# Filling projections placed step by step in a braided attention stage, by VectorE's time instead of TensorE's

## The chip, the cores and the metric

The kernel runs on one core of one Trainium2 chip. The metric is the device time of one execution in microseconds; a kernel is timed several times and the median is compared. The profile that is shown is of one execution.

## The reference, cut to what matters

One decoder layer on 1024 tokens, 16 learned meta tokens ahead of them (T = 1040), all in fp32:

```python
h = h + 0.5 * swiglu(rms_norm(h, ffn1_norm), ffn1_w_in, ffn1_w_out)
u = rms_norm(h, mix_norm) @ w_in            # one combined projection
hq, hf, hi, hg, sq, sk, sv = split(u)       # HGRN2 heads | stick-breaking heads
o_hg = hgrn2(hq, hf, hi, hg, ...)           # 4 heads, 128 x 128 state, blocks of 128
o_sb = stick_breaking(sq, sk, sv, ...)      # 8 heads of 64
h = h + concat[o_hg, o_sb] @ w_out
h = h + 0.5 * swiglu(rms_norm(h, ffn2_norm), ffn2_w_in, ffn2_w_out)
```

A stick-breaking head, for one block of 128 queries:

```python
z = einsum('qd,kd->qk', q, k) * scale
log_keep = where(allowed, log_sigmoid(-z), 0)
suffix = cumsum(log_keep, reverse=True) - log_keep
w = exp(where(allowed, log_sigmoid(z), -inf) + suffix)
o = w @ v
```

An HGRN2 head projects q, f, i (its value) and a gate g, and computes a gated linear recurrence: within a block by products of q and k with the decays between them, between blocks by a state.

## The kernel before, in words

*Stages.* FFN1, then the combined projection up to the columns that the stick-breaking heads need (to 849.5 us of the profiled execution), then the **attention stage** (849.5 to 1119.7), in which the stick-breaking heads are computed and the columns of the HGRN heads are projected between their steps, then the **HGRN stage** (to 1255.8), in which the HGRN heads run between the steps of w_out for the first half of the tokens, then the rest of w_out and FFN2. The first 28 us of the HGRN stage, up to the first w_out step at 1147.3, are the hand-over: the projections that are left over run there beside the first instructions of three heads.

*Number format.* Every big matrix product is done on fp32 operands split in a high and a low part: `product` (L242) issues three matmuls for each 128 rows of the contraction, high by high (L249), high by low (L250) and low by high (L251), into one PSUM tile. One **product step** of a projection is four such triples, 12 matmuls, 512, 256 or 272 columns wide; two steps fill one tile `proj`. A step of w_out is one triple into a tile `wo`.

*Orders.* TensorE's order is written out: it runs its instructions in the order in which the program issues them. The orders of the other engines (VectorE = DVE, ScalarE = ACT, GpSimd = POOL, and SyncE = SP, which issues most DMAs) are set by a scheduler from what the program issues.

*The attention stage.* `sb_jobs` (L1518) yields 32 jobs, 8 heads by 4 pairs of query blocks in the order 0, 6, 2, 4 (the second job of a head is its largest, with blocks 6 and 7). A job consists of three lists of steps:

- *score steps* (`sb_scores`, L1645), one for each piece of up to 456 key columns: TensorE computes `z` (L1664, L1665), ScalarE the sigmoids `keep` and `sig` (L1666, L1667), VectorE a running product over the piece, the scan (L1670), and POOL multiplies it with sig (L1677). `z` has two PSUM buffers.
- *turn steps* (`unit`, `meta`): TensorE transposes up to four 128 x 128 blocks of sig, `flip` (L1515, L1571; two PSUM buffers), and `sb_parts` splits them into a high part by a copy on ScalarE (L1642) and a low part by a difference on VectorE (L1643), tiles `wu` (and `wm` for the meta columns).
- *value steps*: matmuls of `wu` and `wm` with the values `v` into `oacc` (L1592, L1594). `sb_out` writes the job's output away.

`braid` (L1718) sets the order. In slot `at` stand the score steps of job `at`, the turns of job `at - 2` and the values of job `at - 3`. Each slot gets filling steps from `columns` (`hgrn_fill`, L1131): product steps of the HGRN heads' columns, in the order v, f, q, g of each head. Their eviction `use` takes two sigmoids on ScalarE (L1154, L1155) and two operations on VectorE for f, one each (L1162, L1163) for q and g, a copy on ScalarE for v; the results `st` are stored to DRAM (hg_v, hg_k, hg_f, hg_q, hg_g) by DMAs on SP. With a new column its weights `raw` are loaded (L227) and split by a cast on ScalarE (L232) and a difference on VectorE (L234). Before, a slot's filling is 1.22 times the slot's own time on TensorE by the planner's table; it is spread evenly over the slot's places, and every step is sorted by its place.

*The HGRN stage.* What `braid` left of `columns` goes to `rest()`, and `weave` puts the first instructions of HGRN heads between these product steps (it ends with the fill). `hgrn_attend` (L1198) loads vT, KB, QA, F and masks (L1212), turns vT on TensorE (`flip`, evicted by L1233 and L1236 into vm and vr), multiplies QA with KB for the blocks (`lvl`, L1248) into `attn` (L1252, VectorE), scales QA by F (L1249), then goes level by level: KB is multiplied with F (L1270, VectorE), ScalarE copies it into KP (L1277), TensorE multiplies QA with KP (`lvl`, L1283), and VectorE writes the result into attn by a predicated copy (L1291). Behind the levels `op` (L1347, L1351) applies attn to the values, and `onp` (L1367) turns the normed result vT back. The second `weave` puts the heads' remaining steps between the 64 w_out steps of `first_half_of_o`.

The calls in `run()`:

```python
self.braid(jobs, islice(columns, 76), 1.22, 2.0, 3.0)
...
left = list(columns)                      # in rest(): product steps that braid left over
...
self.weave(rest(), heads[:3], 1e6, 1.0, True)
```

Of the kernel before, what the change touches and what calls it, by code (L numbers as in the profile page):

```python
# [49 lines left out]
class Block:  # L50
# [1667 lines left out]
    def braid(self, jobs, fill, share, turn, value):  # L1718


        waiting = []
        owed = 0.0
        at = 0
        while True:
            job = next(jobs, None)
            for lag, steps in zip((0.0, turn, value), job or ()):
                spans = [1.0 if lag == turn else t for t, _ in steps]
                done = 0.0
                for span, (t, f) in zip(spans, steps):
                    waiting.append((at + lag + (done + span / 2) / sum(spans), t, f))  # L1730
                    done += span
            if not waiting:
                break
            now = [x for x in waiting if x[0] < at + 1]
            waiting = [x for x in waiting if x[0] >= at + 1]
            owed += share * sum(t for _, t, _ in now)
            more = []
            while owed > 0:
                step = next(fill, None)
                if step is None:  # L1740
                    break
                more.append(step)
                owed -= step[0]
            now += [(at + (i + 0.5) / len(more), t, f) for i, (t, f) in enumerate(more)]
            for _, _, f in sorted(now, key=lambda x: x[0]):
                f()
            at += 1

    def weave(self, fill, streams=(), total=0.0, work=0.0, brief=False, steady=False):

# [48 lines left out]
    def run(self):  # L1799
# [21 lines left out]
        with ExitStack() as c0:  # L1821
            with ExitStack() as c1:
# [8 lines left out]
                with tc.manual_schedule(engines={nc.tensor.engine}), ExitStack() as c2:  # L1831
# [4 lines left out]
                    turn = self.pool("turn", ctx=c2)  # L1836
# [68 lines left out]
                    def taken(at, step=True):  # L1905
# [14 lines left out]
                    steps = self.fast_in(  # L1920
                        ops, n, a["ffn1_w_in"][0], act1D, 4, ev0, open_ev, None, begin, spare,
                        lambda: next(turning[0], None), late=lambda: next(later, None),
                        taken=taken,
                    )
# [14 lines left out]
                with tc.manual_schedule(engines={nc.tensor.engine}), ExitStack() as c2:  # L1939
# [140 lines left out]
                    loads = {("A12", 7 + m): (m, c_a) for m in range(4)}  # L2080
# [54 lines left out]
                    def project_early(ci, *plan):  # L2135
                        t0, m = CHUNKS[ci]
                        banks = [early_bank(name, ci, tag) for name, _, tag in plan]
                        for k in range(KT):
                            for ps, (_, w, _) in zip(banks, plan):
                                self.product(ps, w, xh, xl, t0, m, [k])  # L2140
                            if k == 3:
                                yield
# [6 lines left out]
                    key = project_early(0, ("k", wk, None))  # L2149
# [5 lines left out]
                    value = project_early(0, ("v", wv, None))  # L2155
# [22 lines left out]
                columns = self.hgrn_fill(xh, xl, pst, hgD)  # L2178
                oH, self.att = [], []

                def tasks():
                    done = []
                    for i in range(4):
                        for x in done[i - 2] if i > 1 else ():
                            yield "join", x
                        done.append(
                            (yield from self.sb_project(i, xh, xl, mixb, mix, (qD, kD, vD)))
                        )
                        if i == 2:
                            next(jobs)  # L2190
                    for t, f in islice(columns, 16):
                        f()
                        yield t

                with tc.manual_schedule(engines={nc.tensor.engine}):
                    cf = ExitStack()
                    fetch = self.pool("fetch", ctx=cf, side="right")
                    jobs = self.sb_jobs((qD, kD, vD, oD), fetch, self.att)
                    with ExitStack() as c2:
                        mixb = self.pool("mixb", ctx=c2)  # L2200
                        mix = self.pool("mix", ctx=c2)
                        self.weave(tasks())
                    with ExitStack() as c2:
                        self.att.append(self.pool("att1", ctx=c2))
                        tag = self.proj_tags[0]
                        self.proj_tags = [self.proj_tags[1]] * 2
                        self.begin = self.pproj.tile([P, 512], F32, tag=tag, name="begin", bufs=1)
                        nc.vector.memset(self.begin, 0.0)
                        nc.vector.tensor_copy(self.begin[:, 1 : P + 1], self.ident[:, ::-1])
                        self.braid(jobs, islice(columns, 76), 1.22, 2.0, 3.0)  # L2210
                    cf.close()
                    self.proj_tags[0] = tag
                    hg_ctx = ExitStack()
                    hg = self.pool("hg", ctx=hg_ctx, side="right")
                    heads = [self.hgrn_attend(h, hg, hgD, oH) for h in range(4)]
                    self.wide = hg.tile([P, 5, 512], U8, name="wide")
                    for i, n in enumerate(LEVELS[:5]):
                        m = self.masks[:, i, :].rearrange("p (b h r) -> p b h r", h=2, r=n)
                        wide = self.wide[:, i].rearrange("p (h c x) -> p h c x", h=2, c=4)
                        for half in range(2):  # L2220
                            for c in range(4):
                                nc.vector.tensor_copy(
                                    wide[:, half, c].rearrange("p (b r) -> p b r", r=n),
                                    m[:, :, 1 - half, :],
                                )
                    for h in range(3):
                        next(heads[h])

                    def rest():
                        left = list(columns)  # L2230
                        for t, f in left[:-1]:
                            f()
                            yield t
                        left[-1][1]()

                    self.weave(rest(), heads[:3], 1e6, 1.0, True)
# [15 lines left out]
            with tc.manual_schedule(engines={nc.tensor.engine}), ExitStack() as cx:  # L2252
# [103 lines left out]
                def turn_next():  # L2356
# [3 lines left out]
                steps = self.fast_in(  # L2360
                    ops, n, a["ffn2_w_in"][0], actD, 2, ev0, open_ev, made,
                    after_opened=after_opened, between=turn_next,
                )
# [10 lines left out]
            with tc.manual_schedule(engines={nc.tensor.engine}), ExitStack() as c1:  # L2374
# [5 lines left out]
                loads = {("A12", 2 * m): (m, 0) for m in range(4)}  # L2380
# [39 lines left out]
```

## Time and profile before

| | us |
|---|---|
| median of 3 runs | 1944.56 (1943.69 to 1945.66) |
| the profiled execution | 1939.29 |
| its span in the trace | 1937.6 |
| attention stage, in the trace | 849.5 to 1119.7 |
| hand-over, up to the first w_out step | 1119.7 to 1147.3 |
| rest of the HGRN stage | 1147.3 to 1255.8 |

How to read the lines that follow. A row of the table by stage has the stretch, its length, then for PE, PEld, DVE, ACT and POOL the busy time and the count of instructions, and at the end the mean granted clock of TensorE (1.00 is full), the mean busy share of the DMA engines and GB/s. A row of the chain of waits, or of one tile's instructions, has its start, its duration, engine, source line, operation and tiles, and in brackets how long the engine had stood idle before it and for what. A row of waits, "PE flip L1515 <- DVE wu L1643: 2.1, 4, 0.9", says who waited for whom, the sum in us, how often, and the longest. A row of the costliest groups has busy time and the mean in ns of one instruction, then the idle time before them and what ended it.

### The profile page before, as it was taken

What the parts mean: (1) busy time and instruction counts of PE and PEld (TensorE: products, weight loads), DVE (VectorE), ACT (ScalarE), POOL (GpSimd) and SP (SyncE); (2) the same over time, 40 slices, a digit from 0 to 9 for tenths busy, and PEclk for the clock granted to TensorE, in tenths of its full rate; (3) what the DMA queues carried; (4) which work ended last, traced back from release to release, by engine and by line L of the source; (5) the groups of instructions that cost most, each with busy time, mean ns of one, the idle gap of its engine ahead of it and who ended that gap; (6) DMA issues with size and microseconds to landing.
All of it is one profiled execution on the core that took longest, in us unless ns stands there. A gap on an engine that the chain in (4) does not pass through costs nothing.

```text
span 1937.6 us, 30264 instructions
## 1 busy us (share of the span) xinstructions
PE 1916.0 (99%) x10637; PEld 1620.2 (84%) x10637; DVE 1393.9 (72%) x2184; ACT 847.8 (44%) x1712; POOL 452.5 (23%) x625
## 2 busy tenths in 40 slices
PE   9999999999999999999999999999999999999999
PEld 7888888888888888889998988888888888888887
DVE  7977778877678666567777776667577767767774
ACT  7523443334444544356666635433223332344443
POOL 3010100101000003133334342210545544530000
PEclk9999999999999999999999999999999999999999
DMA  7266898757966316765454178646544444469463
GB/s 220 89 174 169 249 287 252 234 190 287 383 229 189 126 53 158 173 183 150 135 155 121 59 257 245 163 186 209 172 127 134 133 128 133 129 251 318 143 233 114
DMA packets 381689, 355.55 MB, mean 184 GB/s; under 512 B 129041, under 2 KB 284561, under 8 KB 381537
## 3 DMA queue, kind: packets, MB, share of 16 engines
q1 hardware_dynamic: 360768, 288.98, 49.4%
q0 software_dynamic: 20768, 64.63, 9.6%
q8 instruction: 84, 1.38, 0.3%
q14 instruction: 69, 0.56, 0.1%
HBM read 237.95 MB, written 115.57 MB: 182 GB/s over the span
## 4 chain that ended last, share of the span: by engine, by line
PE 90%; DVE 5%; ACT 2%; DMA 1%; issue 1%; POOL 1%; SPq 0%; DVEq 0%; POOLq 0%; ACTq 0%
PE o L735 22%; PE qb L452 18%; PE qc L452 12%; PE qa L452 12%; PE proj L249 4%; PE proj L251 4%; PE proj L250 4%; PE flip L1515 2%; PE wo L250 1%; PE wo L249 1%; PE wo L251 1%; PE mq L1014 1%; PE oacc L1594 1%; PE oacc L1592 1%; PE z L1665 1%
## 5 line engine op out<-in xcount | busy, mean ns | idle before, releaser
L452 PE MATMUL qb<-T,wh 128*128 128x512 f32 x1056 | 343.8, 390 | 0.3 <-DVE u L484 0.3
L452 PEld LDWEIGHTS qb<-T,wh 128*128 128x128 f32 x1056 | 198.2, 188 | 44.4 <-issue 3.3
L452 PE MATMUL qa<-B,wh 128*128 128x512 f32 x696 | 227.6, 392 | 0.3 <-ACT B L838 0.2
L362 DVE TENSOR_TENSOR wl<-s,wh 128x512 fp32r<-128x512 f32 x160 | 166.0, 1037 | 70.0 <-ACT wh L360 69.1
L249 PE MATMUL proj<-xh,wh 128*128 128x512 f32 (+2 forms) x640 | 212.7, 332 | 1.2 <-ACT kT L1391 0.6
L735 PE MATMUL o<-t,w 128*128 128x512 f32 x924 | 211.9, 390 | 0.0
L251 PE MATMUL proj<-xl,wh 128*128 128x512 f32 (+2 forms) x640 | 209.3, 327 | 0.7 <-DVE xl L1983 0.7
L735 PE MATMUL o<-parts 128*128 128x512 f32 x924 | 209.6, 389 | 0.0
L250 PE MATMUL proj<-xh,wl 128*128 128x512 f32 (+2 forms) x640 | 208.9, 326 | 0.0
L452 PE MATMUL qb<-T,wl 128*128 128x512 f32 x528 | 205.4, 389 | 0.0
L735 PEld LDWEIGHTS o<-t,w 128*128 128x128 f32 x924 | 172.8, 188 | 36.9 <-issue 0.4
L735 PEld LDWEIGHTS o<-parts 128*128 128x128 f32 x924 | 173.4, 188 | 36.0
L360 ACT CAST wh<-s 128x512 fp32r<-128x512 f32 x160 | 99.4, 622 | 187.3 <-PE qb L452 143.7
L452 PEld LDWEIGHTS qa<-B,wh 128*128 128x128 f32 x696 | 130.5, 188 | 29.2 <-issue 1.2
L360 ACT CAST wh<-raw 128x512 fp32r<-128x512 f32 x120 | 74.4, 621 | 144.7 <-PE qc L452 96.7
L452 PE MATMUL qa<-B,wl 128*128 128x512 f32 x348 | 135.5, 389 | 0.0
L249 PEld LDWEIGHTS proj<-xh,wh 128*128 128x128 f32 x640 | 120.9, 189 | 13.0 <-ACT st L1155 1.3
L251 PEld LDWEIGHTS proj<-xl,wh 128*128 128x128 f32 x640 | 120.9, 189 | 11.7 <-DVE xl L1983 1.2
L250 PEld LDWEIGHTS proj<-xh,wl 128*128 128x128 f32 x640 | 121.1, 189 | 9.2
L452 PEld LDWEIGHTS qb<-T,wl 128*128 128x128 f32 x528 | 99.1, 188 | 20.3
L452 PE MATMUL qc<-T,wh 128*128 128x512 f32 x352 | 116.0, 391 | 0.0
L452 PE MATMUL qc<-B,wh 128*128 128x512 f32 x352 | 114.5, 389 | 0.0
(400 smaller groups left out, 3831.0 us busy)
## 6 DMA issues: line engine op xcount, KB each, us to landing
raw<-in_ffn_w_in_dram SPq DMA_DIRECT2D x176, 256.0 KB, 4.0
raw<-in_ffn_w_out_dram SPq DMA_DIRECT2D x112, 256.0 KB, 4.4
w2in<-both SPq DMA_DIRECT2D x28, 512.0 KB, 4.1
raw<-in_w_in_dram SPq DMA_DIRECT2D x25, 512.0 KB, 4.7
ks<-kD SPq DMA_DIRECT2D x32, 260.0 KB, 4.7
wout<-both SPq DMA_DIRECT2D x16, 512.0 KB, 3.7
wh<-w2in SPq DMA_DIRECT2D x27, 256.0 KB, 3.5
wl<-w2in SPq DMA_DIRECT2D x27, 256.0 KB, 3.5
```

Source lines behind the costliest of these rows:

```text
L249: nc.tensor.matmul(ps, wh[:, s], xs, start=k == 0, stop=False)
L250: nc.tensor.matmul(ps, wl[:, s], xs, start=False, stop=False)
L251: nc.tensor.matmul(ps, wh[:, s], xl[:, k, c0 : c0 + n], start=False, stop=k == nk - 1)
L360: nc.scalar.copy(hi, src)
L362: self.block_lo = nc.vector.tensor_sub(lo, src, hi.bitcast(F32))
L452: nc.tensor.matmul(ps, a[:, k, :], b[:, k, :], start=start and k == 0 and i == 0, stop=k == 3 and i == 2, skip_group_check=True,)
L735: nc.tensor.matmul(banks[bank][m], y[:, m * P : (m + 1) * P], z, start=start and at == 0 and e == 0, stop=q == nq - 1 and e == 2, skip_gro ...
L1014: nc.tensor.matmul(ps[at : at + 32, :], self.xm[:, 4 * h + k, :], got[i, h][:, k, :], start=h == 0 and k == 0, stop=h == 1 and k == 3, til ...
L1515: self.nc.tensor.transpose(ps[:m, j, :], src[:, s0 : s0 + m], self.ident)
L1592: nc.tensor.matmul(o[:, c], vj, w[0], start=j == 0, stop=False, skip_group_check=True)
L1594: nc.tensor.matmul(o[:64, c], vj[:, :64], w[1], start=False, stop=end, skip_group_check=True)
L1665: nc.tensor.matmul(z, q, ks[1][:, s0 : s0 + n], start=False, stop=True)
```

## The change

`braid` places the filling in another way. Each score step adds 70 + 2.74 t (t is the step's number in the planner's table, its columns) and each turn step 140 + 1.28 t to what is owed, times `share`; value steps add nothing. These formulas are for VectorE's time. As soon as more is owed than half of the next filling step's own time, that step follows right behind. There is no even spreading any more. What of the 76 steps is not placed when the jobs are through is issued behind the last of them. `share` goes from 1.22 to 0.9.

```diff
         owed = 0.0
         at = 0
+        step = next(fill, None)
         while True:
             job = next(jobs, None)
-            for lag, steps in zip((0.0, turn, value), job or ()):
+            loads = (lambda t: 70 + 2.74 * t), (lambda t: 140 + 1.28 * t), (lambda t: 0.0)
+            for lag, load, steps in zip((0.0, turn, value), loads, job or ()):
                 spans = [1.0 if lag == turn else t for t, _ in steps]
                 done = 0.0
                 for span, (t, f) in zip(spans, steps):
-                    waiting.append((at + lag + (done + span / 2) / sum(spans), t, f))
+                    place = at + lag + (done + span / 2) / sum(spans)
+                    waiting.append((place, share * load(t), f))
                     done += span
             if not waiting:
                 break
             now = [x for x in waiting if x[0] < at + 1]
             waiting = [x for x in waiting if x[0] >= at + 1]
-            owed += share * sum(t for _, t, _ in now)
-            more = []
-            while owed > 0:
-                step = next(fill, None)
-                if step is None:
-                    break
-                more.append(step)
-                owed -= step[0]
-            now += [(at + (i + 0.5) / len(more), t, f) for i, (t, f) in enumerate(more)]
-            for _, _, f in sorted(now, key=lambda x: x[0]):
+            for _, load, f in sorted(now, key=lambda x: x[0]):
                 f()
+                owed += load
+                while step is not None and owed > step[0] / 2:
+                    step[1]()
+                    owed -= step[0]
+                    step = next(fill, None)
             at += 1
+        while step is not None:
+            step[1]()
+            step = next(fill, None)
...
-                        self.braid(jobs, islice(columns, 76), 1.22, 2.0, 3.0)
+                        self.braid(jobs, islice(columns, 76), 0.9, 2.0, 3.0)
```

In number, 74 product steps stood in the attention stage before and 6 were left for `rest()`. Now 75 stand between the jobs' steps, one is drained behind the last, and 4 are left. At the opening of the stage the first product step stands behind the first three score pieces (144, 272 and 456 columns); before, it stood behind the first alone.

TensorE in the middle of the attention stage, between the second and the third job of the first head. `z` are score pieces, `flip` turns, `oacc` values, `proj` products. Before:

```order
L1515 MATMUL flip_8864<-ident_65,sig_8694 128x128 x3
L1664 MATMUL z_8873<-ks_8678,qs_8677 128x144
L1665 MATMUL z_8873<-ks_8679,qs_8677 128x144
L1592 MATMUL oacc_8857<-wu_8745,v_7954 128x256
L1594 MATMUL oacc_8857<-wu_8746,v_7954 64x256
...
L1592 MATMUL oacc_8857<-wu_8779,v_7954 128x256
L1594 MATMUL oacc_8857<-wu_8780,v_7954 64x256
L1515 MATMUL flip_8886<-ident_65,sig_8725 128x128 x4
L249 MATMUL proj_8899<-xh_6535,wh_8612 128x512
```

After:

```order
L1515 MATMUL flip_8883<-ident_65,sig_8710 128x128 x3
L1664 MATMUL z_8892<-ks_8694,qs_8693 128x144
L1665 MATMUL z_8892<-ks_8695,qs_8693 128x144
L249 MATMUL proj_8834<-xh_6535,wh_8631 128x512
...
L1592 MATMUL oacc_8876<-wu_8758,v_7954 128x256
L1594 MATMUL oacc_8876<-wu_8759,v_7954 64x256
...
L1592 MATMUL oacc_8876<-wu_8795,v_7954 128x256
L1594 MATMUL oacc_8876<-wu_8796,v_7954 64x256
L1515 MATMUL flip_8921<-ident_65,sig_8738 128x128 x4
```

The product step stood behind the flip of four blocks; now it stands right behind the score piece, ahead of the values and of that flip.

TensorE at the hand-over. `flip<-vT` and `lvl` are the first instructions of the HGRN heads, told apart by the numbers of vT, QA and KB. Before:

```order
L249 MATMUL proj_12398<-xh_6535,wh_12146 128x512
...
L1515 MATMUL flip_12427<-ident_65,vT_12291 16x128
L1515 MATMUL flip_12430<-ident_65,vT_12291 128x128 x4
...
L249 MATMUL proj_12442<-xh_6535,wh_12146 128x512
...
L1248 MATMUL lvl_12455<-QA_12288,KB_12289 128x128 x4
...
L1515 MATMUL flip_12475<-ident_65,vT_12318 16x128
...
L249 MATMUL proj_12442<-xh_6535,wh_12146 128x512
...
L1283 MATMUL lvl_12647<-QA_12288,KP_12648 128x2x64 x4
L1248 MATMUL lvl_12657<-QA_12315,KB_12316 128x128 x4
...
L249 MATMUL wo_12712<-oT_12630,wh_12626 128x512
```

After:

```order
L249 MATMUL proj_12427<-xh_6535,wh_12039 128x512
...
L1515 MATMUL flip_12597<-ident_65,vT_12320 16x128
...
L1515 MATMUL flip_12612<-ident_65,vT_12347 16x128
...
L1248 MATMUL lvl_12627<-QA_12317,KB_12318 128x128 x4
L1248 MATMUL lvl_12632<-QA_12317,KB_12318 128x128 x4
L1248 MATMUL lvl_12647<-QA_12344,KB_12345 128x128 x4
L1248 MATMUL lvl_12652<-QA_12344,KB_12345 128x128 x4
L1283 MATMUL lvl_12667<-QA_12317,KP_12668 128x2x64 x4
L249 MATMUL wo_12677<-oT_12580,wh_12576 128x512
```

The two product steps that stood between the first head's flips, its lvl and the second head's flips are gone from there; both heads' flips and their lvl of QA and KB follow one another, and the first lvl of QA and KP stands behind them. In VectorE's order the same place reads, before:

```order
L1252 TENSOR_TENSOR attn_12302<-lvl_12455,ident_65 128x512
L1249 TENSOR_TENSOR QA_12288<-QA_12288,F_12290 128x1024
L1252 TENSOR_TENSOR attn_12302<-lvl_12460,ident_65 128x512
L1233 COPY vm_12331<-flip_12475 16x128
L1270 TENSOR_TENSOR KB_12289<-KB_12289,F_12290 128x2x256
```

After:

```order
L1252 TENSOR_TENSOR attn_12331<-lvl_12627,ident_65 128x512
L1249 TENSOR_TENSOR QA_12317<-QA_12317,F_12319 128x1024
L1252 TENSOR_TENSOR attn_12331<-lvl_12632,ident_65 128x512
L1252 TENSOR_TENSOR attn_12358<-lvl_12647,ident_65 128x512
L1249 TENSOR_TENSOR QA_12344<-QA_12344,F_12346 128x1024
L1252 TENSOR_TENSOR attn_12358<-lvl_12652,ident_65 128x512
L1270 TENSOR_TENSOR KB_12318<-KB_12318,F_12319 128x2x256
```

The second head's attn, QA and attn have moved ahead of the first head's KB. On SP, the store of a product step's hg_q now stands between the first head's load of vT and its load of KB.

TensorE at the end of the HGRN stage, between the last `op` and the first `onp`. Before:

```order
L1351 MATMUL op_13657<-vr_13144,attn_13145 128x128
L249 MATMUL wo_13677<-oT_12938,wh_13673 128x512
...
L249 MATMUL wo_13677<-oT_12942,wh_13673 128x512
...
L249 MATMUL wo_13677<-oT_12946,wh_13673 128x512
...
L249 MATMUL wo_13677<-oT_12950,wh_13673 128x512
...
L1367 MATMUL onp_13692<-ident_65,vT_13134 128x128 x4
L1367 MATMUL onp_13700<-ident_65,vT_13134 128x128 x4
```

After:

```order
L1351 MATMUL op_13671<-vr_13160,attn_13161 128x128
L249 MATMUL wo_13661<-oT_12903,wh_13657 128x512
L250 MATMUL wo_13661<-oT_12903,wl_13659 128x512
L251 MATMUL wo_13661<-oT_12905,wh_13657 128x512
L1367 MATMUL onp_13692<-ident_65,vT_13150 128x128 x4
L1367 MATMUL onp_13700<-ident_65,vT_13150 128x128 x4
```

Four steps of w_out stood between them; now one does.

## The prediction

> **What bounds the kernel now.** I read the page's first part and then the table by stage.
>
> ```profile
> PE 1916.0 (99%) x10637; PEld 1620.2 (84%) x10637; DVE 1393.9 (72%) x2184; ACT 847.8 (44%) x1712; POOL 452.5 (23%) x625
> 849.50:1119.70 270.20, 262.35 (x1851) 240.75 (x1850) 201.86 (x327) 179.62 (x462) 97.08 (x140) 1.00 0.45 128
> 1119.70:1147.30 27.60, 26.25 (x157) 22.54 (x157) 17.04 (x58) 8.97 (x15) 16.44 (x36) 1.00 0.89 323
> 1147.30:1255.80 108.50, 105.47 (x695) 90.59 (x694) 75.15 (x138) 54.92 (x153) 29.35 (x44) 1.00 0.75 203
> ```
>
> TensorE is busy for 1916.0 of 1937.6 us, so no change of order can win more than some 20 us in the whole kernel. The attention stage runs from 849.5 to 1119.7 us and leaves TensorE idle for 270.20 - 262.35 = 7.85 us. The hand-over to the HGRN heads (to 1147.3) leaves 1.35 us, the rest of the HGRN stage (to 1255.8) 3.03 us. Only these three stretches have another order; behind them TensorE runs on as before. The attention stage cut at its column changes:
>
> ```profile
> 849.50:858.60 9.10, 7.22 (x35) 4.94 (x33) 6.06 (x12) 6.62 (x18) 1.30 (x4) 1.00 0.82 238
> 858.60:895.00 36.40, 34.95 (x212) 30.38 (x211) 28.81 (x46) 23.09 (x60) 16.27 (x22) 1.00 0.60 154
> 895.00:940.00 45.00, 44.02 (x365) 43.23 (x363) 36.31 (x61) 33.54 (x89) 17.95 (x26) 1.00 0.52 156
> 940.00:981.00 41.00, 39.23 (x238) 34.32 (x237) 26.67 (x44) 23.59 (x59) 12.73 (x22) 1.00 0.53 138
> 981.00:1025.00 44.00, 43.51 (x351) 41.92 (x350) 34.67 (x58) 31.96 (x85) 15.82 (x22) 1.00 0.46 130
> 1025.00:1066.00 41.00, 40.33 (x247) 35.15 (x246) 30.52 (x49) 26.69 (x71) 16.92 (x26) 1.00 0.47 135
> 1066.00:1112.00 46.00, 45.80 (x373) 44.50 (x372) 35.98 (x58) 31.26 (x81) 15.89 (x19) 1.00 0.17 57
> 1112.00:1119.70 7.70, 7.30 (x48) 6.30 (x47) 2.83 (x6) 2.87 (x7) 0.19 (x2) 1.00 0.13 46
> ```
>
> Idle are 1.88 us at the opening, 0.40 in the last 7.7 us and 5.56 between. The stretches whose products are 512 columns wide (858.6, 940, 1025) lose 3.89 of these 5.56. What TensorE waits for there:
>
> ```profile
> PE flip L1515 <- DVE wu L1643: 2.1, 4, 0.9
> PE z L1664 <- ACT sig L1667: 1.9, 4, 0.6
> PE flip L1515 <- POOL sig L1677: 1.6, 2, 1.0
> PE flip L1515 <- DVE wm L1643: 1.0, 2, 0.8
> ```
>
> The waits for wu and wm, and behind POOL's sig the scan, are VectorE that has fallen behind; no single wait is over 1.0 us.
>
> **The change, part by part.**
>
> *A, the middle of the attention stage.* VectorE's work there, by groups of instructions:
>
> ```profile
> L1670 DVE TENSOR_TENSOR_SCAN keep<-keep,begin 128x144 f32<-128x144 f32 (+6 forms) x112 | 97.6, 873 | 12.6 <-ACT keep L1666 8.0 <-POOL keep L1659 1.9 <-ACT sig L1667 1.5
> L1643 DVE TENSOR_TENSOR wu<-flip,wu 128x512 fp32r<-128x512 f32 (+2 forms) x96 | 51.9, 541 | 16.4 <-ACT wu L1642 16.0
> ```
>
> The scans cover 8 x 4736 = 37888 columns, so 2.58 ns each; the differences cover 288 blocks, so 0.18 us each. The slot with the 1952 columns of the largest job and 11 blocks costs VectorE 5.0 + 2.0 = 7.0 us, the slot with 416 columns and 7 blocks 1.1 + 1.3 = 2.4 us. By the planner's formulas the heavy slot got 1.22 x 4.2 = 5.2 us of products and now gets 0.9 x 7.3 = 6.6; the light one got 4.2 and now gets 2.5. Products leave the slots in which VectorE needs no time and go to those in which it is late, and each stands right behind the scan or difference that it covers. No instruction is added or taken away but for one product step (74 steps before, now 75 and one drained at the end), which comes from the stage behind. Bounds: nothing won (the products are still only 2.7 us apart at best), or all 5.56 us and the pipeline's drain behind each wait, some 8 us. I take 4.5, since the waits are short beside a product: **-4.5**.
>
> *B, the opening.* The first product moves from behind the first score piece to behind the third.
>
> ```profile
> 851.38 1.05 ACT L232 CAST wh<-raw 128x1024 fp32r<-128x1024 f32 x1 [1.99 <-DMA raw<-in_w_in_dram]
> 853.04 0.30 ACT L1667 ACTIVATE sig<-z 128x144 f32<-128x144 f32 x1
> 853.39 0.48 PE L1664 MATMUL z<-ks,qs 128*128 128x456 f32 x1 [0.43 <-ACT sig L1667]
> ```
>
> ScalarE stands behind a load of weights until 851.38, so the third piece can't start before 853.39 either way, there being two z buffers. Before, a product filled that time; now TensorE idles for some 3 us. But the product that stood there then stands behind the third piece, and the products behind it come between turns and pieces where the rest of the 1.88 us was lost. **0** (-0.8 to +1).
>
> *C, the close.* The last slots lose two 256-wide products and a 512-wide one between turns, which have two PSUM buffers. The waits of flip for wm above (0.8 at most) are the nearest rows: **+0.8** (0 to 1.5).
>
> *D, the hand-over.* One product step is spent in the attention stage and one is drained behind it. So five steps now follow one another, and none is left between the HGRN heads' first instructions.
>
> ```profile
> 1134.57 1.95 PE L1248 MATMUL lvl<-QA,KB 128*128 128x128 f32 x16
> 1136.35 0.71 PE L1515 MATMUL flip<-ident,vT 128*16 128x128 f32 x5
> 1137.74 0.66 PE L1515 MATMUL flip<-ident,vT 128*128 128x128 f32 x4 [0.68 <-ACT vr L1236]
> 1141.00 1.07 PE L1283 MATMUL lvl<-QA,KP 128*128 128x128 f32 x8
> 1147.30 0.48 PE L249 MATMUL wo<-oT,wh 128*128 128x512 f32 x1
> 1135.66 0.69 DVE L1252 TENSOR_TENSOR attn<-lvl,ident 128x512 f32<-128x512 f32 x1 [3.46 <-PE lvl L1248]
> 1136.55 1.96 DVE L1249 TENSOR_TENSOR QA<-QA,F 128x1024 f32<-128x1024 f32 x1 [0.20 <-PE lvl L1248]
> 1139.23 0.67 DVE L1270 TENSOR_TENSOR KB<-KB,F 128x512 f32<-128x512 f32 x1
> 1139.93 0.68 ACT L1277 COPY KP<-KB 128x512 f32<-128x512 f32 x1 [0.92 <-DVE KB L1270]
> 1143.09 1.31 DVE L1291 COPY_PREDICATED attn<-wide,lvl 128x512 f32<-128x512 uint8 x1
> 1144.84 1.20 DVE L1249 TENSOR_TENSOR QA<-QA,F 128x1024 f32<-128x1024 f32 x1
> ```
>
> Before, KP was there 1140.61 - 1134.57 = 6.0 us after the first lvl, and in those 6.0 us TensorE turned the second head's vT and ran a product, with one wait of 0.68. Now TensorE does both heads' lvl at once (half of the 1.95 us more) and stands before the first lvl<-QA,KP; and VectorE does the second head's attn, QA and attn (0.69 + 1.20 + 0.69) ahead of KB. KP is there 6.0 + 2.6 = 8.6 us after the first lvl, of which some 2 are covered: a wait of 6.5. The second head's KP waits for the predicated copy, two KB and ScalarE behind the first head's lvl, 0.9 + 1.3 + 0.7 + 0.7 + 0.7 = 4.3 us, over 2.6 us of wo and flips: 1.7. With 0.7 for the flips that is 8.9 in place of 1.35: +7.5. Some is given back: TensorE is then later against VectorE, and the 3.03 us it waits for up to 1255.8 shrink; with their drain I take 3.2. **+4.3** (0 to +9). On SP the store of a drained product's hg_q now stands between the load of vT and that of KB and waits for VectorE; KB, QA and F come about a microsecond later, which the five steps cover.
>
> The granted clock is 1.00 in every row above, behind waits of at most 1 us. The Trainium skill (TensorE: Matmul & The Clock Gate, "Part 1: The HAM clock gate") says that TensorE's clock is halved after an idle window of about 3.4 us and comes back after as long a busy one. No row here has such a pause, so the trace neither bears it out nor denies it; by the rows the sum stays as it is, by the rule some 1.7 us come on top, an estimate from that page.
>
> *E, the end of the HGRN stage.* With more of the heads' work in the last interleaving, its 64 wo steps run out sooner: one step instead of four stands between the last op and onp.
>
> ```profile
> 1252.06 0.39 PE L1351 MATMUL op<-vr,attn 128*128 128x128 f32 x2
> 1254.63 0.69 DVE L1361 TENSOR_TENSOR vT<-op,ss 128x512 f32<-128x512 f32 x1
> 1255.06 1.04 PE L1367 MATMUL onp<-ident,vT 128*128 128x128 f32 x8
> ```
>
> vT ends at 1255.32, and onp's second half (from some 1255.5) just doesn't wait. Three steps are 2.1 us, of which nearly all is bared: **+1.9** (0 to 2.1).
>
> Sum: -4.5 + 0 + 0.8 + 4.3 + 1.9 = +2.5 us. On the profiled execution's 1939.29 us that gives 1941.8; this execution lies 5.3 us under the median of the runs, 1944.56, on which it gives 1947.1. A measurement here tells about 0.2% (3.9 us) from no change.
>
> **The rivals.** *Faster:* the stage's waits go entirely (A -8) and the hand-over is mostly taken back, since the HGRN stage's waits are VectorE's (D +2, E +1): -5, 1939.6. For it speaks that 3.89 of the 5.56 us lie where products are widest, and those move most; against it that a wait of 6.5 us can't hide behind 3.03 us of idle time. *Slower, hand-over not taken back:* the order of wo and levels is fixed, and VectorE itself ends its dense stretch later, so D is +7.5: +5.7, 1950.3. It decides once the first lvl<-QA,KP waits over 5 us and the idle time from there to the end of the HGRN stage stays at 3. *Slower by the clock:* the pause of 6.5 us, or the 3 us at the opening, lets the granted clock fall; if it is halved for as long as the long pause was, 3.3 us are lost: +5.8, 1950.4. No row under 1.00 speaks for it, a rule does (above). That the change does nothing is no rival: its order differs in every slot.
>
> **Chances.** My forecast (within 0.2%) 0.47, faster 0.18, hand-over not taken back 0.25, clock 0.10; so slower 0.35. The likeliest case alone spans 1943.5 to 1948.4. The range for 8 in 10 reaches to both sides, 1939.5 to 1952.0.
>
> **What would show it.** A: the stage's idle time in the middle falls from 5.56 to 1 or 2 us, and the waits for wu and wm go. B: one wait of 3 us for sig before the first z of 456 columns. D: a wait of over 5 us before the first lvl<-QA,KP, for ACT KP. E: onp waits some 2 us for vT. Clock: a row under 1.00 behind that wait. I am wrong if the middle's waits stay (new ones behind long runs without a product), or if the first lvl<-QA,KP waits less than 3 us.

## The result and the profile after

| | median, us | runs | against before |
|---|---|---|---|
| before | 1944.12 | 1940.67 to 1945.66 (4) | |
| changed | 1954.39 | 1952.54 to 1958.20 (4) | 1.0062 (1.0050 to 1.0074) |

The change costs 10.3 us by the medians, 12 by the ratio. That is above the range of the prediction, which ended at 1952.0, and on the side to which it had given 0.35. First the page's first part and two stretches of the changed kernel, from the first score piece to the last value step and from there to the last onp; then the same two stretches of the kernel before. The columns are those of the table by stage.

```profile
PE 1920.1 (98%) x10637; PEld 1625.0 (83%) x10637; DVE 1396.1 (72%) x2184; ACT 848.5 (43%) x1712; POOL 451.2 (23%) x625
851.57:1124.00 272.43, 265.85 (x1862) 244.32 (x1861) 203.43 (x326) 181.20 (x462) 99.98 (x140) 0.99 0.45 128
1124.00:1269.90 145.90, 130.83 (x838) 113.39 (x837) 93.46 (x196) 63.74 (x169) 42.94 (x80) 0.98 0.74 220
```

```profile
849.58:1119.70 270.12, 262.27 (x1850) 240.67 (x1849) 201.78 (x326) 179.62 (x462) 97.08 (x140) 1.00 0.45 128
1119.70:1255.80 136.10, 131.72 (x848) 113.12 (x849) 92.19 (x195) 63.90 (x168) 45.79 (x79) 1.00 0.78 227
```

The attention stage holds one product step more (12 matmuls, 2.8 us start to start) and is 2.3 us longer: level, or 0.5 us better. The stretch behind it holds one product step less and is 9.8 us longer: 12.6 us worse, of which 10.7 are idle time of TensorE (145.90 - 130.83 = 15.1 us in place of 4.4). And the granted clock is 0.99 and 0.98 where it was 1.00. The profile before is of an execution (1939.29 us) 5 us under its median, that of the changed kernel (1953.41) 1 us under its own, so the traces differ by more than the medians do. What TensorE waits for behind the attention stage, after and before:

```profile
PE wo L249 <- DMA oT<-oD: 3.7, 1, 3.7
PE wo L249 <- DMA wh<-wout: 3.2, 1, 3.2
PE onp L1367 <- DVE vT L1361: 2.3, 1, 2.3
PE flip L1515 <- DMA vT<-hg_v: 2.2, 1, 2.2
```

```profile
PE knp L1319 <- DVE kms L1313: 1.6, 3, 0.7
PE flip L1515 <- ACT vr L1236: 1.4, 2, 0.7
PE lvl L1283 <- DVE QA L1270: 0.6, 1, 0.6
PE wo L249 <- DMA oT<-oD: 0.5, 1, 0.5
```

Before, no wait there is over 0.7 us, and most are for VectorE and ScalarE; now there are four long ones, three of them for DMAs. The rows of TensorE at these places, and at the opening:

```profile
855.20 0.75 PE L1664 MATMUL z<-ks,qs 128*128 128x456 f32 x1 [2.99 <-ACT sig L1667]
...
1145.83 1.07 PE L1283 MATMUL lvl<-QA,KP 128*128 128x128 f32 x8
1150.65 0.47 PE L249 MATMUL wo<-oT,wh 128*128 128x512 f32 x1 [3.74 <-DMA oT<-oD]
...
1179.09 0.79 PE L249 MATMUL wo<-oT,wh 128*128 128x512 f32 x1 [3.20 <-DMA wh<-wout]
...
1214.20 1.30 PE L1515 MATMUL flip<-ident,vT 128*16 128x128 f32 x9 [2.23 <-DMA vT<-hg_v]
...
1269.52 0.63 PE L1367 MATMUL onp<-ident,vT 128*128 128x128 f32 x4 [2.26 <-DVE vT L1361]
```

The wo matmul at 1179.09 lasts 0.79 us, the same one at 1150.65, still at full clock, 0.47. The table by stage around three of the pauses shows why:

```profile
855.00:856.00 1.00, 0.80 (x2) 0.75 (x3) 1.00 (x3) 0.73 (x3) 0.00 (x0) 0.50 0.59 170
1151.00:1154.50 3.50, 2.91 (x14) 2.24 (x13) 2.17 (x4) 0.78 (x3) 2.67 (x11) 0.59 0.91 274
1179.00:1182.00 3.00, 2.91 (x9) 2.17 (x10) 0.28 (x1) 0.00 (x0) 0.00 (x0) 0.50 0.56 116
```

At the pauses of 2.99, 3.74 and 3.20 us the granted clock falls to 0.50. By the record of the clock each fall takes 1.71 us of full clock away, 5.1 us in all; a part of this passes while TensorE still waits.

### The profile page after: what moved, and what is told of

Same layout as the page of the kernel before. It is cut to its first block, busy times and chain, and to the rows that moved or that the text cites. A ratio compares the mean times of both kernels' runs of the same rounds, so it can differ in the third digit from the quotient of the medians.

```text
span 1951.7 us, 30261 instructions
## 1 busy us (share of the span) xinstructions
PE 1920.1 (98%) x10637; PEld 1625.0 (83%) x10637; DVE 1396.1 (72%) x2184; ACT 848.5 (43%) x1712; POOL 451.2 (23%) x625
## 4 chain that ended last, share of the span: by engine, by line
PE 73%; issue 18%; DMA 3%; DVE 2%; POOL 2%; ACT 1%; SPq 0%; POOLq 0%; DVEq 0%; ACTq 0%
PE o L735 21%; PE qb L452 10%; PE qa L452 8%; PE qc L452 7%; PE proj L249 5%; PE proj L251 5%; PE proj L250 5%; PE flip L1515 2%; PE wo L249 1%; PE wo L250 1%; PE wo L251 1%; PE oacc L1594 1%; PE oacc L1592 1%; PE z L1664 1%; PE z L1665 1%
## 5 line engine op out<-in xcount | busy, mean ns | idle before, releaser
L1677 POOL TENSOR_TENSOR sig<-sig,keep 128x144 f32<-128x144 f32 (+3 forms) x64 | 83.5, 1308 | 142.0 <-DVE keep L1670 96.8
```

The costliest lines, as they stand in the source:

```text
L1677: nc.gpsimd.tensor_mul(sig, sig, keep[:, 1 : nk + 1])
```

## The experiments

Each run is given as its median and its ratio to runs of the kernel before on the same chip, with the 95% interval. The theories: the loss is that of the **cover** (a product step less behind the last value step, while the loads of the HGRN heads run), of the **order** of the heads' instructions behind it, or of the **placement** in the attention stage itself.

### The drain alone

```diff
@@ braid, kernel before
             at += 1
+        for _, f in fill:
+            f()
```

> The kernel before with one thing changed: its two product steps of the 76 that were not placed are issued behind the last job, so that four are left for rest() and the hand-over has the order of the changed kernel (both heads' flips and lvl in a row), but six products still follow the last value step. Theory 1 (cover): from the first head's loads to oT the DMA queue needs some 22 us whatever TensorE does, and the changed kernel lost a product that covered it; here the cover is whole, so the first wo waits for oT less than 1.5 us, the clock stays at 1.00 there, and the time is before +1 to +4 us, what is left being the order of the last interleaving. Theory 2 (order): it is the heads' instructions without products between them that cost, so before +8 to +12 us.

Measured 1954.21 us, 1.0059 (1.0047 to 1.0072), +11.4 us. Cover alone has fallen: six product steps still follow the last value step, and the loss is whole. Its waits behind the attention stage:

```profile
PE flip L1515 <- DMA vT<-hg_v: 2.5, 1, 2.5
PE onp L1367 <- DVE vT L1361: 2.3, 1, 2.3
PE wo L249 <- DMA wh<-wout: 2.2, 1, 2.2
...
PE flip L1515 <- DVE vm L1233: 2.0, 1, 2.0
...
PE wo L251 <- DMA oT<-oD: 1.2, 1, 1.2
...
PE wo L249 <- DMA oT<-oD: 0.7, 1, 0.7
```

The first w_out column waits 0.7 us for oT's high half and 1.2 for its low half, 1.9 in all, where it waited 3.7 in the changed kernel. Cover expected the clock at 1.00 there; it is low from 1149.2 to 1156.0. vT and onp are as late as in the changed kernel, wh waits 2.2 us in place of 3.2, and the falls of the granted clock take 8.5 us in this profiled execution (1956.42 us), where they took 5.1 in that of the changed kernel. The time lies in the range that order gave. So the lost cover is the smaller part, and what the two kernels share, four steps left for `rest()`, is the larger.

### Four products behind the last value step

```diff
@@ run, kernel before
-                        self.braid(jobs, islice(columns, 76), 1.22, 2.0, 3.0)
+                        self.braid(jobs, islice(columns, 76), 1.28, 2.0, 3.0)
```

> The kernel before with share 1.28 in place of 1.22: all 76 product steps stand between the jobs' steps, spread as before, nothing is drained and four are left for rest(). The hand-over has the order of the changed kernel with one product less behind the last value step (four, the changed kernel has five, the kernel before six). Theory 1 (cover): the first wo waits for oT one product (2.8 us) longer than in the changed kernel, about 6 us, the clock falls behind it, and the time is before +10 to +15 us. Theory 2 (order): the wait is no longer than in the changed kernel (3.7 us) and the time is before +8 to +12 us, as in the run with the drain alone.

Measured 1957.93 us, 1.0078 (1.0064 to 1.0091), +15.1 us: at the upper end of cover's range, and outside that of order.

```profile
PE wo L249 <- DMA oT<-oD: 6.2, 1, 6.2
```

With six, five and four product steps behind the last value step the first column of w_out waits 1.9, 3.7 and 6.2 us for oT: 1.9 and 2.5 us more for a step of 2.8. Cover is real as a mechanism, and its price in the changed kernel is the 1.9 us between the first two, besides what the clock loses by it.

### The hand-over put back

```diff
@@ run, changed kernel
-                        self.braid(jobs, islice(columns, 76), 0.9, 2.0, 3.0)
+                        self.braid(jobs, islice(columns, 74), 0.9, 2.0, 3.0)
```

> The changed kernel with 74 product steps given to braid in place of 76: opening and middle as in the changed kernel, the hand-over and all behind it as before (six products behind the last value step, two of them between the heads' instructions). If the hand-over carries the loss, the time is that of before plus the opening (+1.7 us by the two traces) less the middle (-2.2 us): before -3 to +2 us. Rival (the placement in the attention stage itself costs): still before +6 us or more.

Measured 1943.22 us, 1.0001 (0.9992 to 1.0010). The placement in the attention stage stays as in the changed kernel, its opening too, and the net loss is gone: it belongs to the two product steps that `rest()` no longer gets. This run gives back two things at once, the cover and what `rest()` starts; the runs below take them apart.

### The opening put back as well

```diff
@@ braid, the run before this one
-        owed = 0.0
+        owed = 1100.0
```

> The run before this one (74 steps) with owed starting at 1100 in place of 0, so that the first product stands behind the first score piece again, as before. Theory: the 3.0 us wait for sig at the opening and the fall of the granted clock to 0.5 behind it are gone; 1.5 to 3 us less than the run with 74 steps alone, before -1 to -5 us. Rival (the opening is hidden, as I forecast at 0): no difference to the run with 74 steps.

Measured 1943.26 us, 1.0003 (0.9994 to 1.0012): no difference, where the theory forecast 1.5 to 3 us less. The trace shows the clock at 1.00 throughout and the wait at the opening gone, but owed at 1100 moves every product by two fifths of a step, and a new wait of flip for wu (2.4 us) stands at 865. The run can't tell the opening's price from that of the shift.

### oT ahead of the third head's loads

```diff
@@ run, changed kernel
-                    for h in range(3):
+                    for h in range(2):
                         next(heads[h])
...
-                    self.weave(rest(), heads[:3], 1e6, 1.0, True)
+                    self.weave(rest(), heads[:2], 1e6, 1.0, True)
...
                         o = [from_dram(0)]
+                        next(heads[2])
```

> The changed kernel with the loads of the third HGRN head (vT, KB, QA, F, KM, FM, some 2.1 MB) issued behind those of the first w_out weights and oT, not ahead of them; TensorE's order is the same. Theory (the DMA queue bounds the first wo): oT lands some 5 us earlier, the 3.7 us wait of the first wo and the fall of the granted clock behind it (another 1.7 us) are gone: changed kernel -3 to -6 us. Rival (the wait only moves to the third head's flips, whose vT now lands later): no more than 1.5 us less than the changed kernel.

Measured 1956.32 us, 1.0068 (1.0055 to 1.0080): a miss, no gain at all. The first wo no longer waits, as expected, but the rival holds:

```profile
PE flip L1515 <- DMA vT<-hg_v: 8.2, 2, 5.7
```

One step of w_out later TensorE stands 5.7 us for the third head's vT. The loads are one stream that keeps the DMA engines busy (a share of 0.93 to 1.03 in every 5 us from 1130 to 1155); to bring one of them forward moved the wait to another and won nothing.

### Three buffers for the w_out weights

```diff
@@ run, changed kernel
-                    self.weights("wo", 2, 2, c1)
+                    self.weights("wo", 2, 3, c1)
```

> The changed kernel with three buffers in place of two for the w_out weights wh and wl, so that the fifth column's weights are issued before oT's second half and not behind it. Theory (the wait of 3.2 us for wh is a queue place, given by the buffers and by how dense the wo steps stand): that wait and the clock's fall behind it (1.7 us) go, changed kernel -3 to -5 us. Rival (the queue is full there anyway): the wait stays or moves to oT, -1 to +1.

Measured 1950.82 us, 1.0044 (1.0032 to 1.0057), 3.5 us less than the changed kernel by the two ratios (whose intervals overlap a little). The wait for wh is gone: with two buffers that load is issued behind oT's second half (at 1170.3, behind 1164.7), with three ahead of it (1159.7, ahead of 1160.5). The wait for oT is 4.4 us here, and the clock is low for twice as long at it.

### The pace of the w_out steps

The second `weave` deals the 64 w_out steps out in proportion to the heads' work done so far, against a total that it is told, 114850. `rest()` starts the first head once 9000 of its clock are spent. Six steps left over (five of them count, 13680) reach that; four (8208) do not, so the first head's flips and lvl and the second's flips (960 + 3000 + 960) fall to the second `weave`, whose total isn't told of them.

```diff
@@ run, changed kernel
-                        self.weave(first_half_of_o(), lanes, 64 * 650.0 + 4000.0, 114850.0, steady=True)
+                        self.weave(first_half_of_o(), lanes, 64 * 650.0 + 4000.0, 119770.0, steady=True)
```

> The changed kernel with the total work of the second weave told as 119770 in place of 114850 (the 960 + 3000 + 960 of the head steps that are now left to it added), so that the 64 wo steps last to the end: four steps between the last op and onp again. Theory: onp's wait of 2.3 us goes, and since the wo steps stand less densely the waits for wh shrink: changed kernel -2 to -5 us. Rival (the steps at the end are missed earlier): -1 to +1.

Measured 1945.31 us, 1.0016 (1.0007 to 1.0025): 9 us less than the changed kernel by the ratios, more than expected. Its stretch behind the last value step:

```profile
1124.10:1264.30 140.20, 131.46 (x839) 113.92 (x837) 92.06 (x195) 64.03 (x168) 44.26 (x79) 0.98 0.75 220
```

140.2 us in place of 145.9, in a profiled execution of 1947.65 us. Its longest waits there:

```profile
PE flip L1515 <- ACT vr L1236: 3.1, 3, 2.1
PE knp L1319 <- DVE kms L1313: 1.8, 4, 0.6
PE wo L249 <- DMA oT<-oD: 1.8, 1, 1.8
```

wh and onp are gone from the list and oT is halved; at the fourth head's flips 2.1 us go to ScalarE's copy vr, in place of 2.2 to the DMA of vT. What `rest()` starts is as in the changed kernel, so most of what the run with the drain left to order is the pace.

### The clock kept up

```diff
@@ sb_scores and mix_out, changed kernel
+            if self.pieces == 3:
+                tag = self.proj_tags[0]
+                self.warm(self.pproj.tile([P, 512], F32, tag=tag, name="warm", bufs=1), 26)
...
+            if k == 0 and k0 and half == 0 and m in (0, 4):
+                self.warm(ps, 32 if m == 0 else 29)
...
+    def warm(self, ps, n):
+        for i in range(n):
+            t = ps[:, P * (i % 4) : P * (i % 4) + P]
+            self.nc.tensor.transpose(t, self.ident, self.ident)
```

> The changed kernel with transposes of ident that nobody reads put into three waits of TensorE: 26 ahead of the third score piece at the opening, 32 ahead of the first wo and 29 ahead of the fifth w_out column's first wo. They change no other order. Theory (the clock falls to 0.5 for 3.4 us behind each of these three waits, and that costs 1.7 us each): the granted clock stays at 1.00 there, changed kernel -3 to -5.5 us. Rival (what is behind the waits isn't bound by TensorE's clock): -1 to +1.

Measured 1950.42 us, 1.0036 (1.0023 to 1.0050), 5 us less than the changed kernel by the ratios (whose intervals just touch), where 3 x 1.71 = 5.1 was to be had. The third score piece, the first wo and the fifth column's first wo have the transposes ahead of them. The work is the same and 87 transposes more; the clock is 1.00 in the trace up to its end. With the time at half clock behind it, the pause of 2.99 us in the changed kernel costs TensorE 4.4 us, that of 3.20 us 4.8.

### The opening alone

```diff
@@ braid, kernel before
-            for _, _, f in sorted(now, key=lambda x: x[0]):
+            now = [f for _, _, f in sorted(now, key=lambda x: x[0])]
+            if at == 0:
+                held = [f for _, f in more]
+                now = [f for f in now if f not in held]
+            if at == 1:
+                now[1:1] = held
+            for f in now:
                 f()
```

The product of the first slot is held back and put behind the first step of the second, which is the third score piece.

> The kernel before with its first product step moved from behind the first score piece to behind the third, as in the changed kernel; all else as before. Theory of my prediction (the opening costs nothing): before -1 to +1 us. Theory from the trace of the changed kernel (a wait of 3.0 us for sig and the clock at 0.5 for 3.4 us behind it): before +1.5 to +4 us.

Measured 1944.37 us, 1.0006 (0.9997 to 1.0015), +1.0 us: the interval, -0.6 to +2.9 us, reaches into both forecasts. The trace leans to the second: the pause is 2.88 us, the clock falls behind it, and the stretch to the last value step is 2.2 us longer than before.

```profile
850.28:1122.60 272.32, 263.07 (x1850) 241.89 (x1849) 202.08 (x326) 179.48 (x462) 96.15 (x140) 0.99 0.45 127
853.00:857.00 4.00, 3.20 (x8) 2.66 (x9) 3.73 (x8) 2.31 (x8) 0.60 (x3) 0.57 0.61 186
```

### The causes taken out together

The changed kernel with the pace of 119770, three buffers, and transposes at the opening (26) and ahead of the first wo (14); the edits are those above.

> The changed kernel with what the runs before named taken out together: the second weave told 119770 of work, three buffers for the w_out weights, and transposes that nobody reads in the waits at the opening (26) and ahead of the first wo (14). Placement in the attention stage and the five products behind it stay as in the changed kernel. Theory (pacing of the wo steps, the weights' buffers and the clock carry the loss): before -2 to +1.5 us. Rival (the lost product behind the last value step still costs its wait for oT): before +2 to +5 us.

Measured 1943.71 us, 1.0003 (0.9994 to 1.0012). The loss is gone with the changed placement, the drain and the five steps behind the last value step still in place; the rival (+2 to +5) lies outside the interval but for its lower end. The gains of the single runs (9, 3.5 and 5 us) add up to more than the loss: each takes out waits and falls that the others take out too, so no share of the 12 us belongs to one of them alone. The wait for oT isn't gone, it is filled; the trace behind the last value step is still 1.7 us longer than before with a product step less.

```profile
1120.90:1258.70 137.80, 130.49 (x853) 112.55 (x851) 92.82 (x195) 64.03 (x168) 44.08 (x79) 1.00 0.75 224
```

### What the placement is worth by itself

```diff
@@ changed kernel: braid and run
-        owed = 0.0
+        owed = 1100.0
...
-                        self.braid(jobs, islice(columns, 76), 0.9, 2.0, 3.0)
+                        self.braid(jobs, islice(columns, 74), 0.87, 2.0, 3.0)
```

> The changed placement with 74 steps, owed starting at 1100, and share 0.87 in place of 0.9, so that the 74 steps reach up to the last jobs and the hand-over is as before. It asks what the placement by VectorE's time is worth by itself. Theory of my prediction (the waits in the middle go, -4.5 us): before -2.5 to -5 us. Rival (the waits that go are replaced by others, as the runs with 74 steps showed): before -1.5 to +1 us.

Measured 1941.82 us, 0.9995 (0.9987 to 1.0004): not told from before, at the edge of the rival's range. One pause stands in the way, at the place where the run with owed at 1100 had it, and the clock falls behind it:

```profile
866.74 0.52 PE L1515 MATMUL flip<-ident,sig 128*128 128x128 f32 x2 [2.35 <-DVE wu L1643]
```

The last run takes owed at 500 instead, so that the first product stands behind the second score piece, in the opening's own wait:

```diff
@@ braid, the run before this one
-        owed = 1100.0
+        owed = 500.0
```

> The run before (74 steps, share 0.87) with owed starting at 500 in place of 1100: the first product stands behind the second score piece, in the very wait of 2.9 us for sig that the opening has when it stands behind the third, and the products that follow stand a fifth of a step later, so that flip has not to wait 2.4 us for wu at 866. Theory (the placement is worth something once the opening is covered and no pause lets the clock fall): no pause over 1.5 us and the clock at 1.00 in the whole stage, before -2 to -5 us. Rival (the middle's waits are worth nothing): before -1 to +1 us.

Measured **1937.71 us, 0.9977 (0.9968 to 0.9986)**, 4.65 us less than before: faster than both kernels. A part of it is the clock: all 11 executions have a mean granted clock of 1.00, of the 15 of the kernel before beside them only five; the mean of the 11 is 3.9 us under that of these five.

```profile
849.65:1115.80 266.15, 260.93 (x1850) 240.64 (x1849) 202.04 (x326) 180.19 (x462) 98.04 (x140) 1.00 0.46 130
1115.80:1253.30 137.50, 132.06 (x850) 112.90 (x849) 93.14 (x195) 63.81 (x168) 43.13 (x79) 1.00 0.76 225
```

With as many products as before (1850 matmuls) the attention stage is 4.0 us shorter by the traces; the longest wait of TensorE in it is 1.0 us. The stretch behind it, whose order is that of the kernel before, is 1.4 us longer.

## Why the prediction was wrong

*The sum* was +2.5 us, the measurement 10.3 by the medians. By the traces, from the first score piece to the last onp, it is 418.3 against 406.2 us: 12.1.

*A, the middle (-4.5).* Right in direction, too large in size. The stage without its first 9.1 and last 7.7 us, in the changed kernel and in the last run:

```profile
860.67:1116.30 255.63, 252.71 (x1791) 233.39 (x1791) 194.98 (x310) 174.05 (x445) 97.45 (x134) 1.00 0.45 127
858.75:1108.10 249.35, 246.25 (x1771) 228.95 (x1770) 192.41 (x309) 171.01 (x440) 95.91 (x134) 1.00 0.46 129
```

TensorE's idle time there falls from 5.6 us to 2.9 and 3.1; the prediction had 1 or 2. The waits for wu and wm do nearly go: 0.8 us in the changed kernel, where they were 3.1. That the whole stage of the last run is 4.0 us shorter, near the 4.5, is partly luck: its opening, with 0.8 us of idle time in place of 1.9, has a part in it. In the changed kernel the attention stage as a whole, A, B and C together, shows -0.5 in place of the predicted -3.7: the opening takes part of the gain. C by itself was small, as forecast: 0.67 us of idle time in the last 7.7 us, where 0.40 were before.

*B, the opening (0).* The wait of 3 us was foreseen, word for word; the step that failed is that it would be paid back. The idle time of the first 9.1 us grows from 1.9 to 3.0, and the clock falls. The trace with the opening alone has +2.2, of which up to 1.7 are the clock's fall. Its run (+1.0, interval from -0.6 to +2.9) does not settle the size.

*D, the hand-over (+4.3).* The step that failed is the reading of the row of KP at 1139.93, which I took for the first level's KP. It is the second level's. The rows of that copy in the kernel before, and in the changed kernel:

```profile
1128.61 0.85 ACT L1277 COPY KP<-KB 128x512 f32<-128x512 f32 x1 [2.59 <-DMA KB<-hg_k]
...
1139.93 0.68 ACT L1277 COPY KP<-KB 128x512 f32<-128x512 f32 x1 [0.92 <-DVE KB L1270]
```

```profile
L1277 ACT COPY KP<-KB x2: 671/764/856, 1134.6 to 1149.6; 128x512 f32<-128x512 f32 x2
```

The first KP is copied at 1128.61, in the changed kernel at 1134.6, straight from the loaded KB, ahead of the product KB by F; `level` does it in this order. So the first lvl<-QA,KP at 1145.83 waits for nothing, and the wait of 6.5 us that I forecast isn't there. What bounds the place was in none of my rows: the loads. On SP, after:

```profile
1126.84 0.37 SPq L1212 DMA_DIRECT2D vT<-hg_v  x1
1128.31 0.32 SPq L1164 DMA_DIRECT2D hg_q<-st  x1
1128.68 0.42 SPq L1212 DMA_DIRECT2D KB<-hg_k  x1
...
1144.41 5.92 SPq L2270 DMA_DIRECT2D oT<-oD  x8
```

Three heads' tiles, the first weights and oT are one stream of 24 us from its first load to the first wo (1126.84 to 1150.65; before 1123.03 to 1147.30). The DMA share of 0.89 in the row of the hand-over that the prediction quotes said so, and I read past it. I weighed the drained store's microsecond against "the five steps", but not the stream's end against TensorE's.

*E, the end (+1.9).* Right at its place: onp waits 2.3 us. But it was priced as a local matter. The same cause, head steps that fall to the second interleaving, makes every w_out step there stand too early, and that is where wh and the fourth head's vT are waited for. This is the largest error: one wrong pace, seen and taken for 1.9 us, is worth some 9 (the run with 119770), with the falls of the clock that go with its waits.

*The rivals.* The clock came as the rival told, a fall behind a long pause, but three times in place of once: 5.1 us where I had put 3.3 and a chance of 0.10, and at waits that I had not named but for the opening's. The Trainium skill (TensorE: Matmul & The Clock Gate, "Part 1: The HAM clock gate") gives half the clock, and a length of some 3.4 us; half the clock, for 3.41 us, and so 1.71 us lost are what the trace has. The hand-over was indeed not taken back, by other waits than I had named.

## What to carry to other kernels

When filling work is moved between two planners, count what the second one gets, and look for the numbers in it that assume the old amount: a start time that is no longer reached and a total that is no longer true cost more here than everything that the change set out to move. Where the loads of the next stage start with the end of this one, the products behind that end are the cover of the loads, and each one taken from there shows as a wait not much shorter than itself (1.9 and 2.5 us for steps of 2.8). And a change of order can be worth something and still measure nothing until its single worst pause is filled. When a row carries the first stage of a forecast, make sure by what it waited for that it is the instruction that you mean: the row of KP had waited for a product by F, and the first level's copy doesn't.

## What the runs showed of the hardware

I had not expected the clock to fall behind pauses so short. Over the traces of all kernels shown here, from the start of the attention stage to the last onp, TensorE paused 41 times for more than 1.2 us. Behind the 10 pauses of up to 1.62 us the granted clock never fell; behind the 13 of 2.86 us and more it always did; of the 18 between 1.8 and 2.65 us it fell behind 11 (at one of them it was already low). Pauses of 2.27 us did both.

So the length of a pause alone does not decide. In each trace the stretches of low clock begin whole multiples of 3.413 us apart (in the changed kernel at 854.65, 1151.61 and 1178.92: 87 and 8 times 3.413), and each of those looked at here lasts 3.413 us or twice that. (Each trace has one more at the end of the program; it gives the grid where no other does.) Cut on this grid, two pauses of 2.27 us ahead of the same onp look like this, in the run with the drain alone, where the clock fell, and in the run with the clock kept up, where it did not:

```profile
1268.67:1272.08 3.41, 1.15 (x7) 1.07 (x8) 2.70 (x5) 1.62 (x7) 0.86 (x1) 1.00 1.05 398
1272.08:1275.49 3.41, 3.41 (x9) 2.65 (x8) 0.96 (x2) 0.62 (x1) 0.00 (x0) 0.50 1.06 281
```

```profile
1260.31:1263.73 3.42, 2.80 (x22) 2.39 (x21) 0.58 (x1) 1.65 (x8) 1.80 (x3) 1.00 0.97 251
1263.73:1267.14 3.41, 1.76 (x10) 1.58 (x11) 2.38 (x5) 1.35 (x5) 0.73 (x1) 1.00 1.04 394
```

The first pause lies within one window of the grid, which TensorE spends idle for 2.26 us; the second is shared by two, with 0.6 and 1.65 us. Over all 14 traces there are 1690 such windows at full clock from the start of the attention stage to 3 us behind the last onp. In 23 of them TensorE was idle for 1.87 us or more, and behind every one the clock fell; of the other 1667 it fell behind two, with 1.80 and 1.13 us. What in the second of these let it fall is not known. The ends of matmuls are modelled in the trace, so the bound is rough.

A fall takes 1.71 us of full clock, and 21 of the 25 did. Four lasted for two windows, 3.41 us: those at the pauses of 4.36, 5.66 and 6.22 us, and one in the run with the drain alone, which a pause of 2.00 us followed. The "idle window of about 3.4 us" that the prediction quoted from the Trainium skill (TensorE: Matmul & The Clock Gate, "Part 1: The HAM clock gate") agrees with the grid's 3.413 us, but as a length for a single pause it is too long: 1.87 us within one window were enough, and at the opening the clock fell (854.65) while the pause of 2.99 us (to 855.20) still lasted.
